# Three more pairs of projection blocks with seven-product units in a hybrid mixer layer on Trainium2

## The chip, the core and the metric

One core of one Trainium2 chip runs the whole layer in one launch. The metric is the device time in microseconds, the median of repeated runs: 2087.34 us before the change.

## What is computed

The reference is one decoder layer on 256 rows of 2048 columns, in float32:

```
h = x
f1 = (silu(n(h) @ w_gate) * (n(h) @ w_up)) @ w_down      # 2048 -> 5504 -> 2048
h = h + 0.5 * rms_norm(f1)
u = rms_norm(h); proj = u @ w_in                          # 11 parts of w_in's columns
g_q, g_k, g_v, g_out, g_code, h_q, h_f, h_i, h_out, z_gla, z_hgrn = split(proj)
o_gla  = gated_linear_attention(g_q, g_k, g_v, decay(g_code)) * silu(g_out)     # 4 heads
o_hgrn = gated_linear_attention(silu(h_q), 1 - f, h_i, f(h_f)) * silu(h_out)    # 8 heads
merged = sigmoid(z_gla) * (o_gla @ w_branch_gla) + sigmoid(z_hgrn) * (o_hgrn @ w_branch_hgrn)
h = h + rms_norm(merged @ w_out)
h = h + 0.5 * rms_norm(second feed-forward like the first)
```

## The kernel before

The 256 rows are two row blocks t of 128. Every product of float32 matrices is made of three passes in a reduced format (mm3, L145): high part by high part, low by high, high by low. Weights arrive in chunks of two 128-row tiles by 512 columns, by SyncE's (SP's) DMA queue, into a ring of five raw tiles; ScalarE (ACT) copies a chunk to its high part `whi` and VectorE (DVE) subtracts to get the low part `wlo` (split_into, L140), each in a ring of five. A plain 512-column block (`gemm_block`, L151) has eight chunks, each of twelve matmuls of 128x512 on TensorE (PE).

A pair (`gemm_pair`, L319) computes two blocks together. In some of its eight row-tile pairs ("units", `seven`, L255) it replaces eight 128-tile products by seven products of sums, 21 matmuls for 24; DVE forms the weights' sums (`wsum`, `wsuml`), ACT their high parts (`wsumh`). At the end of a pair, shared products are added up (`share`) and added to the results (`close`, L307). A pair occupies all eight PSUM banks once its seven-product units have begun, four for results c and four for shared products p.

The mixer's blocks come in this order before: GQ; CODE with HQ0 (528 columns); the pairs GK/GV0 and GV1/GO0; the plain blocks GO1, HF0, HI0, HO0, HQ1, HF1, HI1, HO1; ZG0, BG0 (branch product of the first attention), ZG1, BG1; the pair ZG2/ZG3 and BG2, BG3; two pairs of ZH; four branch blocks of the second attention; then the output projection. First letters: G and H are the two branches' parts, Z the branch gates.

Other work is put between chunks by a `Side` object (L41): after each twelve matmuls `pump` takes one step of every light generator (transposes, decays `hfT`/`hkT`, dot products `hd`) and, at every second pump, one step of each of the first two heavy ones, the attention chains of t = 0 and 1. An attention chain goes through levels of 1 to 64 rows: small matmuls of qT and kT on PE (L885, L892), then scalings of kT and qT and a masked copy on DVE (L901 to L906), later matmuls with the values, a copy of the state on ACT (L955) and normalised, gated outputs (L967). The attention chains of a branch are appended when its values and gates exist. Every engine runs its instructions in the order that the program fixes; PE's matmuls of a plain chunk stand there as hi, lo, hi passes in turn.

The residual h stays in eight SBUF tiles. After the first layer's settle of h (L492) the mixer reads it again only at its end.

Of the kernel before, what the change touches and what calls it, by code (L numbers as in the profile page):

```python
# [7 lines left out]
F32 = mybir.dt.float32  # L8
# [19 lines left out]
RW = -(-2 * (16 + CB) * 4 // LINE) * LINE // 4  # L28
# [12 lines left out]
class Side:  # L41
# [5 lines left out]

    def __init__(self):
        self.light, self.heavy, self.due = [], [], False

    def _step(self, queue, g):
        try:
            next(g)
        except StopIteration:
            queue.remove(g)
# [5 lines left out]
    def pump(self):  # L61
        for g in list(self.light):
            self._step(self.light, g)
        self.due = len(self.heavy) < 2 or not self.due
        if self.due:
            for g in self.heavy[:2]:
                self._step(self.heavy, g)
# [12 lines left out]
def kernel(ctx: ExitStack, tc: tile.TileContext, a: dict, out: bass.AP):  # L80
# [10 lines left out]
    psum = ctx.enter_context(tc.tile_pool(name="psum", bufs=8, space=bass.MemoryType.PSUM))  # L91

# [9 lines left out]
    h = [[hpool.tile([P, CB], F32, name=f"h{t}_{n}") for n in range(4)] for t in range(NT)]  # L102

# [47 lines left out]
    def gemm_block(w_dram, c0, w, lhs, nkt=KT, held=None, raws=(), ready=()):  # L151
# [5 lines left out]
        nb = -(-w // CB)  # L157
        pss = [[ps_tile(f"mm{t}") for _ in range(nb)] for t in range(NT)]

        def chunk(k0, alloc):  # L160
            if ready:
                return ready.pop(0)
            raw = raws.pop(0) if raws else None
            return wchunk(w_dram[k0 * P:(k0 + 2) * P, c0:c0 + w].rearrange("(k p) c -> p k c", p=P),
                          w, alloc, raw)

        def mm(t, k0, parts):
            for i, part in enumerate(parts):
                kt = k0 + i
                x = lhs(t, kt)  # L170
                for j, ps in enumerate(pss[t]):
                    sl = slice(j * (w // nb), (j + 1) * (w // nb))
                    mm3(ps[:, :w // nb], x, (part[0][:, sl], part[1][:, sl]),
                        kt == 0, kt == nkt - 1)

        if held is None:
            for k0 in range(0, nkt, 2):
# [22 lines left out]
    def operand_sums(x, new_part, out, more=True):  # L200
# [4 lines left out]
        for units in [SUMS] + [(u,) for u in FOUR if more and u not in SUMS]:  # L205
            n = len(units)
# [112 lines left out]
    def gemm_pair(ws, w, lhs, sums, ready=(), following=(), raws=(), sevens=SUMS):  # L319
# [15 lines left out]
        if len(sevens) > len(SUMS):  # L335
# [6 lines left out]
        for u, i in steps:  # L342
# [12 lines left out]
        for i in range(2 if sevens else 0):  # L355
            for t in range(NT):
                b.close(t, i)
        return *[[b.c[t][i] for t in range(NT)] for i in range(2)], ready
# [409 lines left out]
    def mixer(x, rs, ready, following):  # L768
        xl = lhs_of(x)
        w_in = a["w_in"]  # L770
        with ExitStack() as mctx:
# [5 lines left out]
            def blk(s, dt=F32):  # L777
                return b2.tile([P, CB], dt, tag="b", name=nm(s), bufs=31)
# [31 lines left out]

            def transposed(src, dst):
# [4 lines left out]
                nc.scalar.copy(dst, tp)  # L816

            def scaled(ps, sc, s):
                dst = blk(s)
# [8 lines left out]
            def gate(ps, r, normw, width, s):  # L828
                sg = silu(ps, r, blk(s))
# [13 lines left out]
            def dots(q, k, d, row=None):  # L843
# [3 lines left out]
                pr = blk("pr")  # L847
                if row is not None:
                    nc.vector.tensor_tensor(pr, q, row(), op=ALU.mult)
                    q = pr  # L850
                nc.vector.tensor_tensor(pr, q, k, op=ALU.mult)
                nc.vector.tensor_reduce(d, tiles4(pr), AX.X, ALU.add)
# [7 lines left out]
            def attention(t, qT, kT, fT, d, vs, gates, dv, br, b0):  # L860
# [3 lines left out]


# [69 lines left out]
                for b in range(nb):  # L935
                    while t == 1 and (br, b0 + b) not in state:
                        yield
                    o = ps_tile()
                    for j in range(hpb):
# [3 lines left out]
                                         rhs=vs[b][:, cs], start=True, stop=t == 0)  # L943
# [3 lines left out]
                    if t == 0:  # L947
                        kv = ps_tile()
                        for j in range(hpb):
# [3 lines left out]
                                             rhs=vs[b][:, cs], start=True, stop=True)  # L953
# [11 lines left out]
                    for j in range(hpb):  # L965
                        cs = slice(j * dv, (j + 1) * dv)
                        nc.vector.scalar_tensor_tensor(on[:, cs], o[:, cs], r[:, j:j + 1],  # L967
                                                       gates[b][:, cs], op0=ALU.mult, op1=ALU.mult)
# [14 lines left out]
            def branch_bias(row, n):  # L983
                bt = blk("bg")
# [4 lines left out]
            def branch_gate(z, bt):  # L989
                sz = []  # L990
                for t in range(NT):
                    s = blk("sz")
                    nc.vector.scalar_tensor_tensor(s, z[t], rs[t], bt, op0=ALU.mult, op1=ALU.add)
                    nc.scalar.activation(s, s, AF.Sigmoid)
                    sz.append(s)
                return sz

            def gla_decays(code, fT):
# [35 lines left out]
                for g, m in enumerate(ms):  # L1034
                    mv = m.rearrange("p (h t c) -> p h t c", t=NT, c=P)
                    for t in range(NT):
                        nc.scalar.activation(tiles4(fT[t])[:, 2 * g:2 * g + 2, :], mv[:, :, t, :],
                                             AF.Exp)

            def hgrn_gates(y, t, g, fT, kT):  # L1040
# [6 lines left out]
                for i in range(4):  # L1047
# [5 lines left out]
                    lc[:, 4 * g:4 * g + 4].unsqueeze(2).broadcast_to([P, 4, P]), op=ALU.mult)  # L1053

# [24 lines left out]
            def two(sums, c0, c1, ready, *following):  # L1079
# [3 lines left out]
                                 sevens=FOUR if four else SUMS)  # L1083
# [44 lines left out]
            k, v, ready = two(sums, O_GK, O_GV, (), cols(O_GV + CB), cols(O_GO))  # L1128
# [3 lines left out]
            vb, gb = [[scaled(v[t], rs[t], "v") for t in range(NT)]], []  # L1132
            v, go, ready = two(sums, O_GV + CB, O_GO, ready, cols(O_GO + CB))
            vb.append([scaled(v[t], rs[t], "v") for t in range(NT)])
            gb.append([gate(go[t], rs[t], gnorm, 256, "go") for t in range(NT)])
            go = gemm_block(w_in, O_GO + CB, CB, xl, ready=ready)
            gb.append([gate(go[t], rs[t], gnorm, 256, "go") for t in range(NT)])
            for t in range(NT):
# [172 lines left out]
```

## Time and profile before

| quantity | value |
|---|---|
| median of 3 runs | 2087.34 us (2087.27 to 2087.7) |
| profiled execution | 2087.65 us, its span 2085.7 us, mean granted clock 0.999 |
| PE busy | 2075.6 us |
| DVE busy | 1790.7 us, 86% |
| ACT busy | 1207.8 us, 58% |
| weight traffic | 195 GB/s over the span |

The span is the time from the first instruction to the last in the trace; some 2 us of the run's time lie around it. Matmul ends are modelled in the trace, so consecutive start times tell the pace, and a PE that is called busy may still wait inside a row.

### The profile page before, as it was taken

The page shows a single profiled execution, that of the slowest core. Times are in us where ns is not written, and L with a number is a line of the kernel's source. Part 1 is how long each engine was busy: PE and PEld are TensorE (multiplying, and loading weights), DVE is VectorE, ACT ScalarE, POOL GpSimd, SP SyncE. Part 2 cuts the span into 40 slices and gives each one's busy share as a digit, 9 for nine tenths or more (in the row PEclk, how much of TensorE's full clock was granted, in tenths as well). Part 3 has the DMA queues.
Part 4 walks back from the last instruction along what each step waited for, and adds up shares of the span by engine and source line. Part 5 has one row for each costly group of instructions (what it writes and reads, how often), then busy time and mean ns, then how long its engine had stood idle before and what let it go on. Part 6 is the DMA issues. An engine that isn't in the chain of part 4 may idle for free.

```text
span 2085.7 us, 29137 instructions
## 1 busy us (share of the span) xinstructions
PE 2075.6 (100%) x10553; PEld 1730.5 (83%) x10553; DVE 1790.7 (86%) x2116; ACT 1207.8 (58%) x1594; POOL 38.4 (2%) x87
## 2 busy tenths in 40 slices
PE   9999999999999999999999999999999999999998
PEld 7888888898888888888888888888888888898886
DVE  7898999989999889766668897578999989999896
ACT  6555656565666576554545564465655555566563
POOL 1000000000000100000000000010000000000000
PEclk9999999999999999999999999999999999999999
DMA  8566656667667456655565675655655656575663
GB/s 266 184 209 200 213 187 197 209 185 222 216 198 234 150 180 201 183 152 163 167 177 171 214 229 191 207 189 172 219 190 191 208 191 217 166 244 192 204 212 128
DMA packets 198034, 408.22 MB, mean 196 GB/s; under 512 B 17201, under 2 KB 25841, under 8 KB 197890
## 3 DMA queue, kind: packets, MB, share of 16 engines
q1 hardware_dynamic: 193136, 399.70, 61.0%
q10 hardware_dynamic: 4754, 6.66, 1.0%
q8 instruction: 82, 1.34, 0.3%
q14 instruction: 62, 0.51, 0.1%
HBM read 404.20 MB, written 2.10 MB: 195 GB/s over the span
## 4 chain that ended last, share of the span: by engine, by line
PE 97%; DVE 1%; issue 0%; ACT 0%; DMA 0%; POOL 0%; DVEq 0%; POOLq 0%; ACTq 0%
PE c L147 19%; PE c L149 19%; PE c L148 19%; PE mm L147 6%; PE mm L149 6%; PE mm L148 6%; PE p L148 5%; PE p L149 5%; PE p L147 5%; PE ps L379 2%; PE acc L149 1%; PE acc L147 1%; PE acc L148 1%; DVE h L492 0%; PE ps L885 0%
## 5 line engine op out<-in xcount | busy, mean ns | idle before, releaser
L141 ACT ACTIVATE whi<-raw 128x1024 fp32r<-128x1024 f32 (+3 forms) x520 | 541.7, 1048 | 367.7 <-PE mm L148 153.6
L143 DVE TENSOR_TENSOR wlo<-raw,whi 128x1024 fp32r<-128x1024 f32 (+3 forms) x520 | 624.0, 1208 | 145.7 <-ACT whi L141 137.4
L147 PE MATMUL c<-whi,xhi 128*128 128x512 f32 (+1 forms) x1055 | 408.8, 388 | 0.0
L149 PE MATMUL c<-wlo,xhi 128*128 128x512 f32 (+1 forms) x1055 | 406.2, 385 | 0.0
L148 PE MATMUL c<-whi,xlo 128*128 128x512 f32 (+1 forms) x1055 | 406.2, 385 | 0.0
L233 DVE TENSOR_TENSOR wlo<-raw,whi 128x1024 fp32r<-128x1024 f32 (+1 forms) x222 | 259.3, 1201 | 7.8 <-ACT whi L272 4.3
L149 PEld LDWEIGHTS c<-wlo,xhi 128*128 128x128 f32 x1055 | 198.1, 188 | 38.3
L147 PEld LDWEIGHTS c<-whi,xhi 128*128 128x128 f32 x1055 | 198.1, 188 | 37.6 <-ACT xhi L451 0.5
L148 PEld LDWEIGHTS c<-whi,xlo 128*128 128x128 f32 x1055 | 198.2, 188 | 37.3
L233 DVE TENSOR_TENSOR wsuml<-wsum,wsumh 128x1536 fp32r<-128x1536 f32 (+1 forms) x111 | 191.8, 1728 | 36.3 <-ACT wsumh L274 35.9
L147 PE MATMUL c<-whi,hkhi 128*128 128x512 f32 x558 | 217.0, 389 | 0.0
L149 PE MATMUL c<-wlo,hkhi 128*128 128x512 f32 x558 | 216.8, 388 | 0.0
L148 PE MATMUL c<-whi,hklo 128*128 128x512 f32 x558 | 216.7, 388 | 0.0
L272 ACT ACTIVATE whi<-raw 128x1024 fp32r<-128x1024 f32 (+1 forms) x111 | 116.0, 1045 | 169.9 <-DVE raw L233 55.3
L147 PE MATMUL mm<-whi,xhi 128*128 128x512 f32 (+1 forms) x456 | 174.9, 384 | 0.0
L268 ACT ACTIVATE whi<-raw 128x1024 fp32r<-128x1024 f32 (+1 forms) x111 | 115.7, 1042 | 97.9 <-PE c L148 88.3
L149 PE MATMUL mm<-wlo,xhi 128*128 128x512 f32 (+1 forms) x456 | 171.3, 376 | 0.0
L148 PE MATMUL mm<-whi,xlo 128*128 128x512 f32 (+1 forms) x456 | 171.0, 375 | 0.0
L270 ACT ACTIVATE wsumh<-wsum 128x1024 fp32r<-128x1024 f32 (+1 forms) x111 | 115.7, 1042 | 91.0 <-DVE wsum L233 61.8
L233 DVE TENSOR_TENSOR wsum<-raw,raw 128x1024 f32<-128x1024 f32 (+1 forms) x111 | 133.6, 1203 | 20.7 <-DMA raw<-in_ffn_w_down_dram 15.4
L149 PEld LDWEIGHTS c<-wlo,hkhi 128*128 128x128 f32 x558 | 104.8, 188 | 21.6
L147 PEld LDWEIGHTS c<-whi,hkhi 128*128 128x128 f32 x558 | 104.8, 188 | 21.4
(340 smaller groups left out, 3221.5 us busy)
## 6 DMA issues: line engine op xcount, KB each, us to landing
raw<-in_w_in_dram SPq DMA_DIRECT2D x134, 512.0 KB, 3.8
raw<-in_ffn_w_down_dram SPq DMA_DIRECT2D x124, 512.0 KB, 4.8
raw<-in_ffn_w_up_dram SPq DMA_DIRECT2D x97, 512.0 KB, 4.6
raw<-in_ffn_w_gate_dram SPq DMA_DIRECT2D x96, 512.0 KB, 4.7
raw<-in_ffn_w_gate_dram SPq DMA_DIRECT2D x128, 256.0 KB, 3.8
raw<-in_ffn_w_up_dram SPq DMA_DIRECT2D x126, 256.0 KB, 4.0
raw<-in_ffn_w_down_dram SPq DMA_DIRECT2D x96, 256.0 KB, 4.4
raw<-in_w_in_dram SPq DMA_DIRECT2D x68, 256.0 KB, 3.0
```

The source lines that it names most:

```text
L141: last[0] = nc.scalar.activation(hi, src, AF.Copy)
L143: nc.vector.tensor_tensor(lo, src, hi.bitcast(F32), op=ALU.subtract)
L147: nc.tensor.matmul(ps, lhsT=xhi, rhs=whi, start=start, stop=False)
L148: nc.tensor.matmul(ps, lhsT=xlo, rhs=whi, start=False, stop=False)
L149: nc.tensor.matmul(ps, lhsT=xhi, rhs=wlo, start=False, stop=stop)
L233: return nc.vector.tensor_tensor(o, x, y, op=op)
L268: nc.scalar.activation(ahi, ra, AF.Copy)
L270: nc.scalar.activation(hi[:, 0:2, :], wsum[:, 0:2, :], AF.Copy)
L272: nc.scalar.activation(bhi, rb, AF.Copy)
L379: end = nc.tensor.transpose(dst_ps[:, i * P:(i + 1) * P], src[:, i * P:(i + 1) * P], ident)
```

## The change

Three pairs more are made of plain blocks: GO1 with HF0, HI1 with HO1, ZG0 with ZG1. Each has three seven-product units (of the operand sums that exist already), at the steps 6, 8 and 10 of the pair's (`late=True`), so that attention can use PSUM banks in the steps before. In such a pair `side.fast` makes heavy steps come at every pump, and `side.full` stops them once a seven-product unit is next or running. HI0, HO0, HQ1, HF1 stay plain. The pair GO1/HF0 is followed by HI0 with one chunk prepared (`cols(O_HI)`).

Attention chains are appended before their values and gates exist (`attend`); a chain yields `WAITS`, which is not counted as a step, until its inputs are marked as written (`laid`) and until the values and gates of its next part are there. The operand sums for the pairs of four units are formed once more only for the unit that was missing.

To make room, the residual is stored to DRAM (`away`, eight stores of 256 KB on SP's queue, behind GQ's loads and among the first of CODE's), its tiles serve for gates, values and biases meanwhile, and eight loads on ACT's queue bring it back in `merge`. The raw ring's tiles shrink from 1088 to 1024 columns: CODE is loaded and split in sixteen chunks of one 128-row tile by 528. The dot products and gates are formed in place, `blk` has 33 buffers for 31.

Counts: PE issues 27 matmuls of 128x512 fewer; DVE has 56 instructions more (nine seven-product units, three `share`, twelve `close` against what was removed), ACT 34 and SP 34 more.

```diff
+RW = 2 * CB
     def pump(self):
...
+        self.due = self.fast or len(self.heavy) < 2 or not self.due
+        if self.due and not self.full:
+            steps = 0
+            for g in list(self.heavy):
+                steps += self._step(self.heavy, g) != Side.WAITS
+                if steps == 2:
+                    break
...
     def gemm_pair(...)
+        if late:
+            at = range(6, 6 + 2 * len(sevens), 2)
...
+            side.fast = late
+            if any(i is None for _, i in steps[j:j + 2]):
+                side.full = True
...
     def attention(...)
+                while not all(id(x) in laid for x in (qT, kT, fT, d)):
+                    yield Side.WAITS
...
-                    while t == 1 and (br, b0 + b) not in state:
-                        yield
+                    while (t == 1 and (br, b0 + b) not in state) or b >= min(len(vs), len(gates)):
+                        yield Side.WAITS
...
+            for t in range(NT):
+                for n in range(4):
+                    nc.sync.dma_start(away[t][n], h[t][n])
...
+            vs, gates = attend(qT, kT, fT, dd, 256, "g", 0)
...
-            go = gemm_block(w_in, O_GO + CB, CB, xl, ready=ready)
+            go, f, ready = two(O_GO + CB, O_HF, ready, cols(O_HI), late=True)
+            gates.append([gate(go[t], rs[t], gnorm, 256, h[t][len(gates)]) for t in range(NT)])
...
+            vs, gates = hgrn(0, hqs, hqT, f)
+            side.spawn(lc_row(1))
+            vs.append(values(gemm_block(w_in, O_HI, CB, xl, ready=ready), 0))
...
+            v, go, ready = two(O_HI + CB, O_HO + CB, (), cols(O_ZG), cols(O_ZG + CB), late=True)
...
+            szs, ready = two_gates(0, O_ZG, 0, ready, first_of(a["w_branch_gla"], 0), late=True)
...
+                nc.scalar.dma_start(m, away[t][n])
```

**The order on the engines.** Each row is line, operation, result <- operands, shape; the line numbers of the changed program are some 10 to 30 higher. First DVE's queue before, at the start of HI0: `wlo` is the low part of a weight chunk, `lcl` part of the next group's row of bounds, `hfT`/`hkT` are decays and keys of the second branch, `pr` and `hd` its dot products.

```order
L143 TENSOR_TENSOR wlo_8171<-raw_8168,whi_8170 128x1024
L1063 SCALAR_TENSOR_TENSOR lcl_7964<-ident,lc,lch_7963 128x128 x4
L143 TENSOR_TENSOR wlo_8189<-raw_8186,whi_8188 128x1024
L1049 TENSOR_SCALAR hfT_7949<-hfT_7949,lc,lb 128x128 x4
L1051 TENSOR_TENSOR hkT_7951<-hkT_7951,lc 128x512
L1049 TENSOR_SCALAR hfT_7950<-hfT_7950,lc,lb 128x128 x4
L1051 TENSOR_TENSOR hkT_7952<-hkT_7952,lc 128x512
L849 TENSOR_TENSOR pr_8017<-hq_6432,lcr_6845 128x512
L849 TENSOR_TENSOR pr_8021<-hq_6433,lcr_6845 128x512
L851 TENSOR_TENSOR pr_8017<-pr_8017,hk_7957 128x512
L851 TENSOR_TENSOR pr_8021<-pr_8021,hk_7959 128x512
L852 TENSOR_REDUCE hd_7961<-pr_8017 128x4
```

In the change DVE's queue at the start of HI0, from the row after the first `hfT` and `hkT`; `kT`/`qT` are scaled for the attention of the first branch, and `wlo_8271` is the low part of HI0's third chunk.

```order
L1076 TENSOR_SCALAR hfT_8138<-hfT_8138,lc,lb 128x128 x4
L1078 TENSOR_TENSOR hkT_8140<-hkT_8140,lc 128x512
L874 TENSOR_TENSOR hk_8145<-hk_8145,lcr_6911 128x512
L872 TENSOR_TENSOR hk_8147<-hq_6443,hk_8147 128x512
L875 TENSOR_REDUCE hd_8149<-hk_8145 128x4
L874 TENSOR_TENSOR hk_8147<-hk_8147,lcr_6911 128x512
L928 TENSOR_TENSOR kT_7219<-kT_7219,tot_7611 128x8x32
L875 TENSOR_REDUCE hd_8150<-hk_8147 128x4
L931 TENSOR_TENSOR qT_6438<-qT_6438,tot_7611 128x8x32
L928 TENSOR_TENSOR kT_7220<-kT_7220,tot_7633 128x8x32
L931 TENSOR_TENSOR qT_6439<-qT_6439,tot_7633 128x8x32
L153 TENSOR_TENSOR wlo_8271<-raw_8268,whi_8270 128x1024
```

The two splits that stood ahead of the decays are down to one (further up, ahead of `lcl`); the products are now in `hk`; attention's scalings and then the split of HI0's third chunk come behind them all.

PE's queue in the same place of the change, from the end of HI0's second chunk: `whi_8270` and `wlo_8271` are the parts of the third chunk, `L919` the small matmuls of attention's levels 32 and 64.

```order
L1097 MATMUL ps_8223<-lcl_8152,ones 128x512
L919 MATMUL ps_8228<-qT_6438,kT_7219 32x32 x8
L919 MATMUL ps_8248<-qT_6439,kT_7220 32x32 x8
L157 MATMUL mm_1699_8161<-whi_8270,xhi_1311_6092 128x512
L158 MATMUL mm_1699_8161<-whi_8270,xlo_1312_6093 128x512
L157 MATMUL mm_1700_8162<-whi_8270,xhi_1326_6187 128x512
L158 MATMUL mm_1700_8162<-whi_8270,xlo_1327_6188 128x512
L919 MATMUL ps_8304<-qT_6438,kT_7219 64x64 x4
L919 MATMUL ps_8311<-qT_6439,kT_7220 64x64 x4
L159 MATMUL mm_1699_8161<-wlo_8271,xhi_1311_6092 128x512
```

Before, the twelve matmuls of a chunk stood together there; now four high passes are taken out ahead, and the matmuls of level 64, which read what DVE scaled, stand ahead of the first low pass.

The second place is ACT's queue at the state copy of the second branch's first group, before (in the block HO0 to HQ1) and in the change (in the pair HI1/HO1). `whi` is the high part of a weight chunk.

```order
L141 ACTIVATE whi_9449<-raw_9447 128x1024
L933 COPY ke_9316<-ps_9311 128x512
L141 ACTIVATE whi_9467<-raw_9465 128x1024
L141 ACTIVATE whi_9503<-raw_9501 128x1024
L955 COPY state_9364<-ps_9359 128x512
L961 ACTIVATE sq_9366,oss_9367<-ps_9354 128x128 x4
```

```order
L151 ACTIVATE whi_9519<-raw_9517 128x1024
L1072 ACTIVATE hfT_9254<-ps_9290 128x512
L1073 ACTIVATE hkT_9256<-ps_9290 128x512
L1072 ACTIVATE hfT_9255<-ps_9302 128x512
L1073 ACTIVATE hkT_9257<-ps_9302 128x512
L982 COPY state_9324<-ps_9319 128x512
```

Ahead of the copy of the state stood weight copies; now a weight copy and the four activations of the next group's decays do.

## Rows read from the trace of the kernel before

**Rows 1.** The page of the profiled execution: busy time of each engine with its share of the span, and the chain that ended last, by engine.
```profile
PE 2075.6 (100%) x10553; PEld 1730.5 (83%) x10553; DVE 1790.7 (86%) x2116; ACT 1207.8 (58%) x1594; POOL 38.4 (2%) x87
...
PE 97%; DVE 1%; issue 0%; ACT 0%; DMA 0%; POOL 0%; DVEq 0%; POOLq 0%; ACTq 0%
```

**Rows 2.** Timeline of TensorE in the pair GK/GV0, the first matmul of a seven-product unit and the first after its 21: start us, duration us, line, matmul.
```profile
757.95 0.39 PE L147 MATMUL p<-whi,xhi 128*128 128x512 f32 x1
...
762.71 0.39 PE L147 MATMUL c<-whi,xhi 128*128 128x512 f32 x1
```

**Rows 3.** Busy time by windows: stretch, its length, then PE, PEld, DVE, ACT, POOL busy us (instructions), granted clock, DMA share, GB/s. The mixer's projections from GK to the end of the branches; the pair GV1/GO0; a pair of the first feed-forward layer with four seven-product units.
```profile
743.20:1304.40 561.20, 561.19 (x3577) 462.20 (x3576) 441.68 (x613) 311.61 (x459) 12.15 (x22) 1.00 0.61 184
786.90:830.90 44.00, 44.00 (x199) 36.53 (x199) 40.12 (x42) 27.82 (x39) 0.00 (x0) 1.00 0.63 197
181.60:222.20 40.60, 40.60 (x184) 33.68 (x183) 38.90 (x39) 23.06 (x27) 0.00 (x0) 1.00 0.60 192
```

**Rows 4.** Timeline of ScalarE in the plain block HF0, with what ended the idle time ahead of it.
```profile
863.53 1.06 ACT L141 ACTIVATE whi<-raw 128x1024 fp32r<-128x1024 f32 x1 [1.66 <-PE mm L148]
```

**Rows 5.** Groups of instructions in 743.2 to 1304.4 us: line, engine, operation, shape, count | busy us, mean ns | idle before.
```profile
L233 DVE TENSOR_TENSOR wsuml<-wsum,wsumh 128x1536 fp32r<-128x1536 f32 x16 | 28.0, 1753 | 7.7 <-ACT wsumh L274 7.6
L233 DVE TENSOR_TENSOR wsum<-raw,raw 128x1024 f32<-128x1024 f32 x16 | 19.5, 1221 | 1.2 <-DMA raw<-in_w_in_dram 0.9
L233 DVE TENSOR_TENSOR c<-c,psum 128x512 f32<-128x512 f32 x20 | 13.0, 690 | 0.0
L233 DVE TENSOR_TENSOR psum<-psum,p 128x512 f32<-128x512 f32 (+1 forms) x15 | 12.9, 859 | 0.3
L233 DVE TENSOR_TENSOR raw<-wsum,raw 128x512 f32<-128x512 f32 x16 | 11.0, 691 | 0.4
```

**Rows 6.** Timeline of DVE after the pair GV1/GO0: closes, weight splits, gates.
```profile
830.41 1.41 DVE L233 TENSOR_TENSOR c<-c,psum 128x512 f32<-128x512 f32 x2
...
834.60 1.40 DVE L825 SCALAR_TENSOR_TENSOR go<-c,r,go 128x512 f32<-128x512 f32 x2
...
837.12 2.35 DVE L143 TENSOR_TENSOR wlo<-raw,whi 128x1024 fp32r<-128x1024 f32 x2
```

**Rows 7.** Timeline of ScalarE at the start of HI0.
```profile
877.19 0.67 ACT L820 ACTIVATE y<-mm,r 128x512 f32<-128x512 f32 x1
...
879.98 1.05 ACT L141 ACTIVATE whi<-raw 128x1024 fp32r<-128x1024 f32 x1
880.92 0.58 ACT L1045 ACTIVATE hfT<-ps 128x512 f32<-128x512 f32 x1
```

**Rows 8.** Timeline of DVE at the start of HI0, in the order of its queue.
```profile
879.62 1.13 DVE L1063 SCALAR_TENSOR_TENSOR lcl<-ident,lc,lch 128x128 fp32r<-128x128 f32 x4
...
882.20 1.12 DVE L1049 TENSOR_SCALAR hfT<-hfT,lc,lb 128x128 f32<-128x128 f32 x4
...
885.56 1.28 DVE L849 TENSOR_TENSOR pr<-hq,lcr 128x512 f32<-128x512 f32 x2
...
887.97 1.26 DVE L852 TENSOR_REDUCE hd<-pr 128x4 f32<-128x512 f32 x2
889.16 0.41 DVE L901 TENSOR_TENSOR kT<-kT,tot 128x256 f32<-128x256 f32 x1
889.49 0.41 DVE L904 TENSOR_TENSOR qT<-qT,tot 128x256 f32<-128x256 f32 x1
...
890.76 1.21 DVE L143 TENSOR_TENSOR wlo<-raw,whi 128x1024 fp32r<-128x1024 f32 x1
891.89 0.41 DVE L901 TENSOR_TENSOR kT<-kT,tot 128x256 f32<-128x256 f32 x1
```

**Rows 9.** Timeline of one early attention step in HF0 (PE, then DVE), and the transposes of 743.2 to 1304.4 as a group.
```profile
863.65 0.74 PE L885 MATMUL ps<-qT,kT 128*32 128x16 f32 x64
864.18 0.42 DVE L901 TENSOR_TENSOR kT<-kT,fT 128x256 f32<-128x256 f32 x1 [1.04 <-PE ps L885]
...
865.79 1.22 DVE L143 TENSOR_TENSOR wlo<-raw,whi 128x1024 fp32r<-128x1024 f32 x1
...
L379 PE MATMUL ps<-ident,on 128*128 128x128 f32 x32 | 4.3, 272 | 0.0
```

**Rows 10.** Timeline around a state copy of the second branch: the state's matmuls on PE, and the matmuls that use its copy.
```profile
1010.88 1.06 PE L952 MATMUL ps<-hv,ke 128*128 128x128 f32 x8
...
1012.71 0.40 PE L945 MATMUL ps<-state,hqT 128*128 128x128 f32 x2
```

**Rows 11.** The last settle of the residual on DVE and the first matmul of CODE on PE.
```profile
701.47 0.74 DVE L492 SCALAR_TENSOR_TENSOR h<-c,r,h 128x512 f32<-128x512 f32 x1
...
718.77 0.28 PE L147 MATMUL mm<-whi,xhi 128*128 128x264 f32 x1
```

**Rows 12.** TensorE's first matmuls, one at the usual pace, its last matmul, and two windows after it (columns as in the table of windows; the granted clock is the third figure from the end).
```profile
1.29 4.21 PE L1251 MATMUL ps<-idle 128*128 128x512 f32 x9 [1.29 <-POOL idle L1246]
...
9.39 0.39 PE L149 MATMUL c<-wlo,xhi 128*128 128x512 f32 x1
...
2076.85 0.39 PE L149 MATMUL c<-held,hkhi 128*128 128x512 f32 x1
...
2081.00:2082.00 1.00, 0.00 (x0) 0.00 (x0) 1.00 (x3) 0.00 (x0) 0.00 (x0) 1.00 0.60 225
2082.00:2083.00 1.00, 0.00 (x0) 0.00 (x0) 0.51 (x1) 0.00 (x0) 0.00 (x0) 0.80 1.02 379
```

More of the change, by code (lines that the diff above doesn't have):

```diff
@@ L41 @@
 class Side:
+    WAITS = "waits"
     def __init__(self):
-        self.light, self.heavy, self.due = [], [], False
+        self.light, self.heavy, self.due, self.full = [], [], False, False
+        self.fast = False
     def _step(self, queue, g):
         try:
-            next(g)
+            return next(g)
         except StopIteration:
@@ L102 @@
     h = [[hpool.tile([P, CB], F32, name=f"h{t}_{n}") for n in range(4)] for t in range(NT)]
+    away = [[dram.tile([P, CB], F32, name=f"away{t}_{n}") for n in range(4)] for t in range(NT)]
     nhalf = const.tile([P, 4], F32, name="nhalf")
@@ L157, in gemm_block @@
         nb = -(-w // CB)
+        step = 2 // nb
         pss = [[ps_tile(f"mm{t}") for _ in range(nb)] for t in range(NT)]
@@ L205, in operand_sums @@
         for units in [SUMS] + [(u,) for u in FOUR if more and u not in SUMS]:
+            if units[0] in out:
+                continue
             n = len(units)
@@ L317, in first_of, with gemm_pair @@
         return chunk
-    def gemm_pair(ws, w, lhs, sums, ready=(), following=(), raws=(), sevens=SUMS):
+    def gemm_pair(ws, w, lhs, sums, ready=(), following=(), raws=(), sevens=SUMS,
+                  late=False):
         raws = list(raws)
@@ L357, in gemm_pair @@
                 b.close(t, i)
+        side.full = side.fast = False
         return *[[b.c[t][i] for t in range(NT)] for i in range(2)], ready
@@ L809, in mixer, with mark @@
                 rq.append(r)
+            laid = set()
+            def mark(*tiles):
+                laid.update(id(x) for x in tiles)
             def transposed(src, dst):
@@ L983, in branch_bias @@
             def branch_bias(row, n):
-                bt = blk("bg")
+                bt = blk("sz") if row else h[0][n]
                 nc.scalar.dma_start(
@@ L987, in branch_bias, with branch_gate @@
                 return bt
[L989 to L995, printed above, removed]
+            def branch_gate(z, bt, s=None):
+                sz = [bt, s or blk("sz")]
+                for t in (1, 0):
+                    nc.vector.scalar_tensor_tensor(sz[t], z[t], rs[t], bt, op0=ALU.mult, op1=ALU.add)
+                    nc.scalar.activation(sz[t], sz[t], AF.Sigmoid)
                 return sz
@@ L1038, in gla_decays @@
                                              AF.Exp)
+                mark(*fT)
             def hgrn_gates(y, t, g, fT, kT):
@@ L1077, in cols, with two @@
                 return first_of(w_in, c0)
-            def two(sums, c0, c1, ready, *following):
+            def two(c0, c1, ready, *following, late=False):
                 four = len(sums) > len(SUMS) and c1 != O_ZH + 3 * CB
                 return gemm_pair([(w_in, c0), (w_in, c1)], CB, xl, sums, ready, following,
-                                 sevens=FOUR if four else SUMS)
+                                 sevens=FOUR if four else SUMS, late=late)
             qs = [scaled(q[t], rq[t], "q") for t in range(NT)]
@@ L1126, in mixer, with attend @@
             side.spawn(lc_row(0))
-            k, v, ready = two(sums, O_GK, O_GV, (), cols(O_GV + CB), cols(O_GO))
+            def attend(qT, kT, fT, dd, dv, br, b0):
+                vs, gates = [], []
+                for t in range(NT):
+                    side.heavy.append(attention(t, qT[t], kT[t], fT[t], dd[t], vs, gates, dv, br, b0))
+                return vs, gates
+            for t in range(NT):
+                for n in range(4):
+                    nc.sync.dma_start(away[t][n], h[t][n])
+            k, v, ready = two(O_GK, O_GV, (), cols(O_GV + CB), cols(O_GO))
             ks = [scaled(k[t], rs[t], "k") for t in range(NT)]
```

126 lines of the change are left out of this document (59 added, 67 removed).

## The prediction

> **What bounds the kernel now.** The page's first part and its chain say TensorE (PE): it is busy for the whole span and holds 97% of the chain [rows 1]. That view cannot show slack, so I went on to start times. In a seven-product unit the first of 21 matmuls of 128x512 starts at 757.95 and the next unit's first at 762.71: (762.71 - 757.95)/21 = 0.227 us each [rows 2]; a plain chunk of twelve takes 2.72 us. No view of PE's waits names anything in mid-kernel, so each matmul taken out is worth 0.227 us, as long as the other engines keep up. The table of windows tells how near they are: in the mixer's projections VectorE (DVE) works 441.68 of 561.20 us, but 40.12 of 44.00 in the pair GV1/GO0 [rows 3]. What keeps PE fed through DVE's uneven work is a lead: the weight copies on ScalarE (ACT) wait for PE to give back a ring slot [rows 4], so four chunks, 4 x 2.72 = 10.9 us, lie split ahead of PE in a plain block.
>
> **The change part by part.** *Fewer matmuls.* Three pairs with three seven units each save 3 x 3 x 3 = 27 matmuls (24 products become 21 in a unit): 27 x 0.227 = 6.1 us. This is on the path everywhere.
>
> *More DVE work.* A unit adds a sum, two half sums and a long split: 1.22 + 2 x 0.69 + 1.75 = 4.35 us [rows 5]; nine are 39.2. Twelve closes at 0.69 are 8.3, nine sums of shared products at 0.86 are 7.7: 55.2 us in all, less one formation of operand sums. It hides beside PE: 441.68 + 55.2 is still below 561.20 less 6.1. So on average nothing is lost; a loss can only come where DVE's work bunches up and the lead is short.
>
> *Place one, the start of HI0.* A pair uses up the lead: its last closes on DVE wait for its last matmul on PE. Call that moment E. After the pair GO1/HF0 comes HI0, with one chunk split at E and the rest behind other work. DVE's queue (first place of the order) is, from the end of the last close at E + 0.8: two gates (four instructions, 834.60 to 837.12, 2.52) [rows 6], the split of the second chunk 1.13, the four lcl 1.13, and one hk product 0.60 [rows 8], which makes E + 6.2. ACT delivers what these need in time: after a weight copy (1.05) and the first y (0.67) its second y, hk and lch take 877.19 to 879.98, 2.8, and a weight copy and hfT, 879.98 to 881.50, another 1.5 [rows 7]: E + 6.0. Then follows what stood together in the kernel before from 882.20 to 890.76 [rows 8]: the decays, 882.20 to 885.56, 3.36; the other three of four products, which took 885.56 to 887.97, 1.8; two reductions to 889.16, 1.2; and four scalings of an attention level at 0.33, 1.3. That is 7.7, so E + 13.9; and only then comes the split of chunk three, 1.13 (890.76 to 891.89): E + 15.0. In the kernel before the same group held up no one: its 8.6 us lay under the lead of 10.9. Now PE has, after E, chunk one 2.72, chunk two 2.72 and a third of chunk three 0.91, eight transposes at 4.3/32 = 0.13, two ones-products at 0.23 and 16 small matmuls of attention, of which 64 took 0.74 [rows 9], some 1.8 more: 8.2, and with its bubbles it stands at about E + 8.4 before matmuls that need those scalings, and then before the split. The wait is 15.0 - 8.4 = **6.6 us**. Bounds: 3 if DVE is a chunk earlier, 8 if the second chunk's split is late too. I take 6.6, since every term is a row of the same instruction.
>
> *The state copy.* In the pair HI1/HO1 the small matmuls that use the attention state follow the copy of it on ACT. Before, 1.83 us from 1010.88 to 1012.71 were enough from the state's own matmuls to the first that uses the copy, and PE filled them [rows 10]; now a weight copy and four activations stand ahead of it on ACT (second place of the order): 1.05 + 4 x 0.58 = 3.4 us [rows 7]. PE's work in between covers what it did and some more; I take 1.3 of it as uncovered (0 to 3.4). The first branch's state stands behind one weight copy and one activation: 0.6 (0 to 1.6).
>
> *Attention inside the pairs.* Late pairs take a step of both chains at every chunk until the units come, 1.6 us of DVE by the rows from 864.18 to 865.79 [rows 9], beside the previous pair's gates and closes. The second step in GO1/HF0 and the one in ZG0/ZG1 each reach PE before DVE has scaled: 0.8 and 0.85 (0 to 2.7, one chunk). At the start of GK/GV0 and of BG0 I find 0.3 each.
>
> *What is hidden.* The residual goes to DRAM on SP's queue, eight stores, ahead of most weight loads of CODE. They wait for the settles of h, done at about 702.2 [rows 11]; CODE starts on PE at 718.8 [rows 11], 16 us later, and only its first two half chunks are loaded ahead of the last stores. No row shows such a store; eight of 256 KB at the 184 GB/s of the mixer [rows 3] would fill 11.4 us, less than the 16, so I cost them at nothing (0 to 3, a chunk, if they start late). The reloads on ACT's queue come with the merge, which ends with the branches at 1304; the residual is used from 1383.7 on. CODE in sixteen half chunks has the same matmuls, and the products in place the same operations.
>
> *Sum.* -6.1 + 6.6 + 1.3 + 0.6 + 0.8 + 0.85 + 0.6 = +4.65. The profiled execution (2087.65, of which 2085.7 span) is 0.3 above the median of 2087.34; put on the median, 2087.34 + 4.65 gives **2092.0 us**. The bounds of the waits, 3 (HI0 alone) to 8 + 3.4 + 1.6 + 2.7 + 2.7 + 0.6 = 19, give 2084 to 2100. A difference of 0.2% (4.2 us) is about what a measurement of this kernel can tell.
>
> **The rivals.** *The clock falls in the HI0 wait.* At the end of the kernel PE's last matmul starts at 2076.85, and the granted clock is 1.00 in each row to 2082 and 0.80 in the next [rows 12]; that is an idle time as long as the 5.5 us that PE would spend before its small matmuls at HI0. [...] At the kernel's start nine matmuls take 4.21 us, 0.47 each in place of 0.227 [rows 12], and by 9.39 they are at full rate; half rate over 4 to 6 us costs 2 to 3. That gives 2094 to 2097. Against it: the wait is at the edge, and is broken by the eight small matmuls.
>
> *Only the large wait is real; not slower.* The waits besides HI0 (4.15 in sum) each hang on PE reaching one copy or scaling within a chunk of it. One queue decides them: if ACT holds its copies when PE frees the slot, as [rows 4] show in plain blocks, PE's preceding chunk (2.72) covers them all. Then 2087.34 - 6.1 + 6.6 = 2087.8. The deciding point is a sum of waits of 6.1 + 4.2 = 10.3: mine is 10.75, so little is needed. With HI0's wait at its lower bound too, 2085.
>
> *The cover holds.* If DVE kept its splits ahead at HI0, as it did before with the same 8.6 us, only some small waits would be left: 2081 to 2084, faster. For it: the four-seven pair runs at 38.90 us of DVE in 40.60 with no wait [rows 3]. Against it: in that pair's block nothing but splits follows the closes, and DVE runs its queue in the order written.
>
> *DVE becomes the bound of the new pairs,* or the trip of h delays weights: the GV1/GO0 pair's 40.12 of 44.00 plus a third unit's 4.35 exceeds what PE takes; every pair could lose 1 to 4 us beyond the lead it enters with: above 2097.
>
> **How the numbers follow.** Forecast (2089.5 to 2094.5, centre 2092) 0.40; clock falls 0.18; only the large wait 0.25; cover holds 0.12; DVE bound 0.05. Faster by over 0.2% (below 2083.2) is most of the cover's case: 0.12. Slower by over 0.2% (above 2091.5) is 0.24 of the forecast's 0.40, the clock's 0.18 and DVE's 0.05: 0.47. The rest, 0.41, is within. The range 2083.5 to 2096.5 leaves out about 0.1 below and 0.08 above.
>
> **What would show it.** In the changed profile, 27 fewer 128x512 matmuls; at the start of HI0 a gap of 5 us or more in PE's start times, with DVE busy on hfT, hkT, hk and hd, and no weight split for some 10 us; a gap of about 1 us before the state's matmuls in HI1/HO1; the granted clock at 1.00 beside the gap (the forecast) or lower behind it (the rival). Wrong would be: no gap at HI0, which leaves only the saved 6.1; or gaps spread over the pairs with DVE at 100%.

## The result and the profile after

| | before | after |
|---|---|---|
| median of 12 runs each | 2087.61 us (2087.27 to 2088.11) | 2092.18 us (2091.0 to 2093.08) |
| ratio after to before | | 1.0021, 95% interval 1.0013 to 1.0029 |
| profiled execution, its span | 2087.65, 2085.7 us | 2091.0, 2089.2 us |

The change makes the kernel slower by 4.6 us; 2092.0 had been forecast. The profiled execution of after is the shortest of its twelve runs, so the trace shows a little less than the usual loss.

The page's first part shows PE busy for less time, DVE for more, both in a longer span [rows 1]:

```profile
PE 2073.3 (99%) x10526; PEld 1725.2 (83%) x10526; DVE 1834.0 (88%) x2172; ACT 1219.7 (58%) x1620; POOL 38.2 (2%) x87
```

The windows of after (columns as in [rows 3]): the mixer's stretch, DVE now 486.36 where it was 441.68, and then the start of HI0 cut where PE's state changes.

```profile
743.20:1304.40 561.20, 555.20 (x3535) 454.94 (x3535) 486.36 (x664) 323.41 (x476) 12.09 (x22) 1.00 0.61 188
...
887.50:892.00 4.50, 0.26 (x2) 0.08 (x2) 4.50 (x10) 4.36 (x15) 0.00 (x0) 1.00 0.00 0
892.00:893.00 1.00, 0.92 (x12) 0.81 (x13) 1.00 (x3) 0.98 (x5) 0.00 (x0) 0.89 0.03 8
893.00:896.00 3.00, 2.96 (x12) 2.34 (x11) 3.00 (x5) 0.59 (x2) 0.00 (x0) 0.50 0.34 65
896.00:897.00 1.00, 1.00 (x5) 0.84 (x4) 1.00 (x2) 0.00 (x0) 0.00 (x0) 0.90 1.07 387
```

PE works 0.26 us in the 4.5 us from 887.5, DVE all of them; afterwards the granted clock reads 0.89, 0.50 and 0.90; behind 897 it is 1.00 again. PE's timeline there (start, duration, line, matmul) shows the same:

```profile
878.76 0.39 PE L157 MATMUL mm<-whi,xhi 128*128 128x512 f32 x1
...
887.29 0.40 PE L158 MATMUL mm<-whi,xlo 128*128 128x512 f32 x1
891.92 1.77 PE L919 MATMUL ps<-qT,kT 128*64 128x64 f32 x16 [4.24 <-DVE qT L931]
893.73 0.80 PE L159 MATMUL mm<-wlo,xhi 128*128 128x512 f32 x1
894.32 0.63 PE L157 MATMUL mm<-whi,xhi 128*128 128x512 f32 x1
894.75 0.63 PE L158 MATMUL mm<-whi,xlo 128*128 128x512 f32 x1
...
896.34 0.39 PE L158 MATMUL mm<-whi,xlo 128*128 128x512 f32 x1
```

878.76 is E of the prediction, the first matmul of HI0. The last high pass ahead of the wait starts at 887.29 and is over for the pace at 887.52, E + 8.8 (8.4 forecast); the small matmuls of level 64 start at 891.92; the first low pass, which needs `wlo_8271`, starts at 893.73, E + 15.0 (15.0 forecast). From 894.32 to 896.02 matmuls start 0.43 us apart, behind 896.34 0.23 us. DVE's queue in the same stretch is the list of the forecast, with the answers to [rows 6] and [rows 8]:

```profile
878.96 0.70 DVE L243 TENSOR_TENSOR c<-c,psum 128x512 f32<-128x512 f32 x1 [0.45 <-PE c L159]
879.57 1.40 DVE L849 SCALAR_TENSOR_TENSOR h<-c,r,h 128x512 f32<-128x512 f32 x2
...
882.08 1.22 DVE L153 TENSOR_TENSOR wlo<-raw,whi 128x1024 fp32r<-128x1024 f32 x1
883.22 1.13 DVE L1091 SCALAR_TENSOR_TENSOR lcl<-ident,lc,lch 128x128 fp32r<-128x128 f32 x4
884.27 0.68 DVE L872 TENSOR_TENSOR hk<-hq,hk 128x512 f32<-128x512 f32 x1
884.87 1.11 DVE L1076 TENSOR_SCALAR hfT<-hfT,lc,lb 128x128 f32<-128x128 f32 x4
...
887.52 0.68 DVE L1078 TENSOR_TENSOR hkT<-hkT,lc 128x512 f32<-128x512 f32 x1
888.13 0.68 DVE L874 TENSOR_TENSOR hk<-hk,lcr 128x512 f32<-128x512 f32 x1
...
890.53 0.41 DVE L928 TENSOR_TENSOR kT<-kT,tot 128x256 f32<-128x256 f32 x1
...
892.13 0.41 DVE L931 TENSOR_TENSOR qT<-qT,tot 128x256 f32<-128x256 f32 x1
892.46 2.35 DVE L153 TENSOR_TENSOR wlo<-raw,whi 128x1024 fp32r<-128x1024 f32 x2
```

Lines left out are of the same kinds. The reader is to see that each instruction begins as the one ahead of it ends (to within 0.1 us), and that no split of a weight chunk stands between 882.08 and 892.46. The view of PE's waits (line, what it waited for, us, times, longest) names the rest; before, it named the start of the kernel alone:

```profile
PE ps L919 <- DVE qT L931: 4.2, 1, 4.2
...
PE ps L972 <- ACT state L982: 0.8, 1, 0.8
PE p L157 <- ACT lcr L1099: 0.7, 1, 0.7
PE ps L397 <- DVE hq L849: 0.2, 1, 0.2
```

Two of them stand where the forecast had little or nothing: 0.7 behind the copy of `lcr` on ACT (in the pair GK/GV0), and 0.8 at a state copy (in a branch block, not in HI1/HO1).

### The profile page after: what moved, and what is told of

It is laid out like the page before. It is cut to its first block, busy times and chain, and to the rows that moved or that the text cites. A ratio compares the mean times of both kernels' runs of the same rounds, so it can differ in the third digit from the quotient of the medians.

```text
span 2089.2 us, 29267 instructions
## 1 busy us (share of the span) xinstructions
PE 2073.3 (99%) x10526; PEld 1725.2 (83%) x10526; DVE 1834.0 (88%) x2172; ACT 1219.7 (58%) x1620; POOL 38.2 (2%) x87
## 4 chain that ended last, share of the span: by engine, by line
PE 96%; DVE 2%; DMA 1%; issue 1%; ACT 0%; POOL 0%; SPq 0%; DVEq 0%; POOLq 0%; ACTq 0%
PE c L157 21%; PE c L159 21%; PE c L158 21%; PE p L157 5%; PE p L159 5%; PE p L158 5%; PE mm L159 4%; PE mm L157 4%; PE mm L158 4%; PE ps L397 2%; PE acc L157 1%; PE acc L159 1%; PE acc L158 1%; DVE wlo L153 1%; PE ps L912 0%
## 5 line engine op out<-in xcount | busy, mean ns | idle before, releaser
L153 DVE TENSOR_TENSOR wlo<-raw,whi 128x1024 fp32r<-128x1024 f32 (+3 forms) x510 | 602.6, 1191 | 113.5 <-ACT whi L151 111.7
L157 PE MATMUL c<-whi,xhi 128*128 128x512 f32 (+1 forms) x1184 | 461.0, 390 | 0.1
L159 PE MATMUL c<-wlo,xhi 128*128 128x512 f32 (+1 forms) x1184 | 457.0, 386 | 0.0
L158 PE MATMUL c<-whi,xlo 128*128 128x512 f32 (+1 forms) x1184 | 456.7, 386 | 0.0
L159 PEld LDWEIGHTS c<-wlo,xhi 128*128 128x128 f32 x1184 | 222.3, 188 | 43.9 <-DVE wlo L153 0.3
L157 PEld LDWEIGHTS c<-whi,xhi 128*128 128x128 f32 x1184 | 222.3, 188 | 42.8 <-ACT xhi L469 0.6
L158 PEld LDWEIGHTS c<-whi,xlo 128*128 128x128 f32 x1184 | 222.4, 188 | 42.2 <-issue 0.3
L158 PEld LDWEIGHTS c<-whi,hklo 128*128 128x128 f32 x558 | 104.7, 188 | 21.5
L157 PE MATMUL mm<-whi,xhi 128*128 128x512 f32 (+1 forms) x264 | 98.7, 374 | 0.0
L159 PE MATMUL mm<-wlo,xhi 128*128 128x512 f32 (+1 forms) x264 | 96.9, 369 | 0.0
```

The source lines that it names most:

```text
L153: nc.vector.tensor_tensor(lo, src, hi.bitcast(F32), op=ALU.subtract)
L157: nc.tensor.matmul(ps, lhsT=xhi, rhs=whi, start=start, stop=False)
L158: nc.tensor.matmul(ps, lhsT=xlo, rhs=whi, start=False, stop=False)
L159: nc.tensor.matmul(ps, lhsT=xhi, rhs=wlo, start=False, stop=stop)
```

## The experiments

Every run stands beside runs of the kernel before on the same chip, whose median was 2087.7 to 2087.8. The intervals of the ratios are some 0.0009 to either side (2 us), so a difference under 2 us between two runs rests on the traces as much as on the times. E stands below for the first matmul of HI0 of the run in question.

**Is it the order at HI0?** The dot products of the second branch's first group are taken two (t = 0) and four pumps (t = 1) later; nothing else changes:

```diff
-            def dots(q, k, d, row=None):
+            def dots(q, k, d, row=None, later=0):
                 yield
                 yield
+                for _ in range(later):
+                    yield
...
+                for j, (q, k, d) in enumerate(zip(qs, ks, ds)):
+                    side.spawn(dots(q, k, d, row, 2 * j + 2 if s == "hd0" else 0))
```

> All three pairs stay; the dot products of the second branch's first group (four products, two reductions, 3.6 us of DVE) are taken two and four pumps later. Theory A: the order of DVE's queue is the whole matter; the split of HI0's third chunk comes by E + 5.7 and that of the fourth by E + 11.6, where PE arrives at about E + 11.1, so the wait falls from 6.2 to under 1 us and the clock stays at full rate: 2083.5 to 2085.5. Theory B: DVE has the same work, so the wait moves to the next chunks or to HO0: 2090 or more.

Measured: 2085.77 us, ratio to before 0.9991 [0.9982, 1.0000], 6.4 us less than the change itself. On DVE the split of chunk three now precedes the decays, and PE's twelve matmuls of that chunk run on. DVE's and then PE's timeline of this run:

```profile
882.11 1.22 DVE L153 TENSOR_TENSOR wlo<-raw,whi 128x1024 fp32r<-128x1024 f32 x1
...
884.30 1.22 DVE L153 TENSOR_TENSOR wlo<-raw,whi 128x1024 fp32r<-128x1024 f32 x1
885.43 1.11 DVE L1078 TENSOR_SCALAR hfT<-hfT,lc,lb 128x128 f32<-128x128 f32 x4
...
889.70 0.42 DVE L933 TENSOR_TENSOR qT<-qT,tot 128x256 f32<-128x256 f32 x1
890.03 1.22 DVE L153 TENSOR_TENSOR wlo<-raw,whi 128x1024 fp32r<-128x1024 f32 x1
```

```profile
889.96 0.39 PE L158 MATMUL mm<-whi,xlo 128*128 128x512 f32 x1
890.28 1.15 PE L921 MATMUL ps<-qT,kT 128*64 128x64 f32 x16
891.35 0.50 PE L159 MATMUL mm<-wlo,xhi 128*128 128x512 f32 x1
```

The small matmuls wait 0.1 us and the low pass comes right behind them. The whole loss at HI0 is gone with the same work on DVE: the order is the cause, and the rival that the wait would only move on falls. No view of PE's waits names HI0 any more. The time is 0.3 above theory A's range; the waits that are left in mid-kernel are 1.1 at a state copy, 0.7 behind `lcr` and 0.2 for `hq`. More of them below.

**Taking more out of the way.** As above, with the dot products four and six pumps later and the decays of both row blocks later as well:

```diff
+                    side.spawn(dots(q, k, d, row, 2 * j + 4 if s == "hd0" else 0))
...
             def hgrn_gates(y, t, g, fT, kT):
                 yield
+                for _ in range(2 * t + 1 if g == 0 else 0):
+                    yield
```

> All three pairs stay; the dot products come four and six pumps later, the decays of t = 0 one pump and of t = 1 three pumps later. Theory A: no wait at HI0 at all; 2083 to 2085, no better than the run with late dot products alone by more than 0.5 us. Theory B: 2090 or more, since the same DVE work has to be done before HO0 ends.

Measured: 2085.87 us, 0.9992 [0.9983, 1.0000]. That is 0.9 above theory A's range, but no better than the run before it, as theory A said and far from theory B: with the dot products out of the way nothing was left to win at HI0.

**What is the clock's part?** Seventeen matmuls are put on PE where it stands idle:

```diff
+                    if br == "g" and t == 0 and c == 64:
+                        warm = ps_tile("warm")
+                        for _ in range(17):
+                            nc.tensor.matmul(warm, lhsT=ones, rhs=x[0][0][:, 0:4, :]...)
```

> Seventeen extra matmuls of 128x512 into a spare PSUM tile stand on PE where it waits at HI0, 17 x 0.227 = 3.9 us of the 4.4 us gap; their result is not used. Theory A with the lower clock as a part of the loss: the granted clock stays at 1.00 after the wait, the 1.3 us of half-rate matmuls (more in most runs, by their lower mean clock) is won back: 2089.5 to 2091, and the runs differ by less than the 2 us they differ by in the changed kernel. Rival (the clock costs nothing): 2092, or 2092 to 2093 if the extra matmuls get in the way.

Measured: 2090.78 us (2089.88 to 2091.43), 1.0012 [1.0004, 1.0021], 1.4 us less than the change. The timeline of PE and the windows of this run:

```profile
888.75 4.13 PE L909 MATMUL warm<-xhi,ones 128*128 128x512 f32 x17
893.17 1.32 PE L924 MATMUL ps<-qT,kT 128*64 128x64 f32 x16 [0.29 <-DVE qT L936]
894.88 0.50 PE L159 MATMUL mm<-wlo,xhi 128*128 128x512 f32 x1 [0.40 <-DVE wlo L153]
895.22 0.39 PE L157 MATMUL mm<-whi,xhi 128*128 128x512 f32 x1
```

```profile
892.00:893.00 1.00, 0.88 (x4) 0.38 (x2) 1.00 (x4) 1.00 (x5) 0.00 (x0) 1.00 0.00 0
893.00:896.00 3.00, 2.42 (x21) 2.02 (x22) 3.00 (x6) 1.81 (x8) 0.00 (x0) 1.00 0.03 8
```

The low pass waits as before for DVE's split, but the clock reads 1.00 from 892 to 896, where it was 0.89 and then 0.50 in the change, and the matmuls behind the wait start 0.23 us apart from 895.22 on, where the change's start 0.43 apart. By the medians of these two runs the clock costs 1.4 us of the 6.4, DVE's order 5. The difference of 1.4 lies within the intervals, so the traces decide: from E to the first matmul of HI1/HO1 the change takes 114.73 us (878.76 to 993.49), this run 113.62 (879.87 to 993.49) and the run with late dot products 108.49 (878.78 to 987.27). By them the clock costs 1.1 and the order 5.1. The profiled execution of this run is as long as that of the change all the same (2091.1 and 2091.0 us), since it lost 1.1 us ahead of E, where the two kernels are the same. In the trace of the change 4.4 us pass from 887.52 to 891.92, and 1.81 us to the low pass where the run with late dot products takes 1.07: again 5.1 for the order. The runs spread over 1.6 us where the change's spread over 2.1, which is no clear difference.

**The first pair undone.** GO1 and HF0 are plain blocks:

```diff
-            go, f, ready = two(O_GO + CB, O_HF, ready, cols(O_HI), late=True)
+            go = gemm_block(w_in, O_GO + CB, CB, xl, ready=ready)
...
+            vs, gates = hgrn(0, hqs, hqT, gemm_block(w_in, O_HF, CB, xl))
```

> GO1 and HF0 are plain blocks again; the pairs HI1/HO1 and ZG0/ZG1, the early attention and the residual's trip stay. Theory A (the loss is one wait at the start of HI0, made by DVE's queue behind a pair with one chunk split, and the lower clock after it): the wait of 6.2 us and some 1.3 to 2.5 us of half-rate matmuls go, 9 matmuls (2.0 us) come back, so 2085.5 to 2086.5 and no gap over 1 us at HI0. Theory B (the new pairs give DVE more work than fits, the wait only shows first at HI0): a gap of several us opens in a later block and the time stays above 2090.

Measured: 2087.8 us, 1.0002 [0.9993, 1.0010]. The wait at HI0 is gone, though DVE's burst is not: 11.4 us pass there from one weight split to the next, more than the 10.4 (882.08 to 892.46) of the change. DVE's timeline:

```profile
884.58 1.23 DVE L153 TENSOR_TENSOR wlo<-raw,whi 128x1024 fp32r<-128x1024 f32 x1 [1.50 <-ACT whi L151]
...
896.00 1.22 DVE L153 TENSOR_TENSOR wlo<-raw,whi 128x1024 fp32r<-128x1024 f32 x1
```

Behind plain blocks the chunks that lie split ahead of PE cover it. So the short lead behind the pair is as much a part of the cause as the order: take away either, and the wait is gone. The time, however, is 1.3 above the upper end of theory A's range. The trace names one reason, a wait that the change does not have, in the pair HI1/HO1: the first small matmuls of the second branch's second group wait there for DVE (timeline of DVE, ScalarE and PE):

```profile
1004.10 0.67 DVE L875 TENSOR_REDUCE hd<-hk 128x4 f32<-128x512 f32 x1
1004.69 1.28 DVE L897 TENSOR_TENSOR hqT<-hqT,hfT 128x512 f32<-128x512 f32 x2
...
1005.51 0.45 PE L912 MATMUL ps<-hqT,hkT 128*32 128x16 f32 x32 [1.45 <-DVE hqT L897]
```

In the change the same matmuls stand in the same pair, but later: they start at 1012.78, 6 us behind DVE's scaling at 1006.19. Without the first pair the first group's attention begins sooner (932.46 for 947.16), and the second group's then comes right behind the scaling. So a wait in a later block, of which theory B spoke, did come, but of 1.5 us and not of several. Without that 1.5 the time would lie in theory A's range.

**What does each other pair bring?** On top of the late dot products, HI1/HO1 and then ZG0/ZG1 are made plain again:

```diff
-            v, go, ready = two(O_HI + CB, O_HO + CB, (), cols(O_ZG), cols(O_ZG + CB), late=True)
-            vs.append(values(v, 1))
-            gates.append(gates_of(go, 1))
+            vs.append(values(gemm_block(w_in, O_HI + CB, CB, xl), 1))
+            gates.append(gates_of(gemm_block(w_in, O_HO + CB, CB, xl), 1))
+            ready = ()
```

> As the run with late dot products (2085.8), but HI1 and HO1 are plain blocks. Theory A: the pair costs no wait of its own, so nine matmuls come back and nothing else: 2085.8 + 2.0 = 2087.8. Theory B (pairs filled with attention steps are bound by DVE): part of the 2.0 was never won, 2086 to 2087.

Measured: 2086.79 us, 0.9995 [0.9986, 1.0004], 1.0 more than with the pair, in theory B's range.

```diff
-            szs, ready = two_gates(0, O_ZG, 0, ready, first_of(a["w_branch_gla"], 0), late=True)
...
+            for i in range(2):
+                szs.append(branch_gate(gemm_block(w_in, O_ZG + i * CB, ...), bts[i], h[1][i]))
...
```

> As the run with late dot products (2085.8), but ZG0 and ZG1 are plain blocks. Theory A: nine matmuls come back, and the wait for the state copy near the branch block (1.2 us there) stays or falls with the new place of the attention steps: 2086.6 to 2087.8. Theory B: 2085.5 to 2086.5.

Measured: 2086.57 us, 0.9994 [0.9985, 1.0003], 0.8 more than with the pair, between the ranges of the two theories. In both traces PE's wait at the second branch's state copy, 1.1 us with late dot products, is gone, and so it is in the run without the first pair; in the run without ZG0/ZG1 one of 0.6 at the first branch's state has come. So that wait stands only where all three pairs do, and what a plain block gives back is a wait for ScalarE; neither trace shows a pair that DVE holds up. For HI1/HO1 2.0 - 1.1 = 0.9 fits the 1.0; for ZG0/ZG1 2.0 - 1.1 + 0.6 = 1.5 does not fit the 0.8. With intervals of 2 us the times do not settle what each pair brings.

**The other parts alone.** First the residual's trip and CODE's half chunks in the kernel before:

```diff
-RW = -(-2 * (16 + CB) * 4 // LINE) * LINE // 4
+RW = 2 * CB
...
+        step = 2 // nb
...
+                    nc.sync.dma_start(away[t][n], h[t][n])
...
+                nc.scalar.dma_start(h[t][n], away[t][n])
```

> The kernel before with only two parts of the change: the residual's trip to DRAM and back (its tiles are not used for anything else meanwhile) and CODE in sixteen half chunks with the smaller ring tiles. Prediction's theory: both are hidden, 2087.4 to 2088. Theory C, formed on the changed kernel's trace: the half chunks halve the lead that ScalarE has at the end of CODE, and the waits at the start of GK/GV0 (0.3 us for the transposes of hq, 0.85 us behind the copy of lcr) are theirs: 2088.4 to 2089.2, with both waits in the trace.

Measured: 2089.66 us, 1.0008 [0.9999, 1.0017], 0.5 above theory C's range and 1.7 above that of the prediction's theory. Of the two waits that theory C named, the one behind `lcr` is in the trace (1.0 us) and the one for the transposes of `hq` is not. Then the half chunks alone, the first two of these edits:

> The kernel before with CODE in sixteen half chunks and the smaller ring tiles alone, no trip of the residual. Theory C (the 1.9 us of the run with both parts are the half chunks': ScalarE enters GK/GV0 later and PE waits behind the copy of lcr): 2089.0 to 2089.8, with the wait of about 1.1 us at the fourth product of the first seven-product unit of GK/GV0. Rival D (the stores and reloads delay weight loads): 2087.5 to 2088, no such wait.

Measured: 2089.6 us, 1.0010 [1.0001, 1.0018], in theory C's range. And the trip alone, the last two:

> The kernel before with the residual's trip to DRAM and back alone, CODE in eight chunks as before. Theory C: hidden, 2087.5 to 2088. Rival D: 2089 to 2089.8.

Measured: 2087.6 us, 0.9999 [0.9990, 1.0008], in theory C's range. The trip is free as far as these times can tell, the half chunks cost 1.9 us. In the run with the half chunks ScalarE's queue is late from the end of CODE on (its last copy of CODE, the first high part of a weight sum, the row of `lcr`; then PE's wait):

```profile
735.68 0.65 ACT L141 ACTIVATE whi<-raw 128x528 fp32r<-128x528 f32 x1 [0.81 <-PE mm L148]
...
748.45 1.04 ACT L268 ACTIVATE wsumh<-wsum 128x1024 fp32r<-128x1024 f32 x1
...
759.47 1.28 ACT L1035 ACT_TABLE_LOAD   x1
...
762.01 0.56 ACT L1069 COPY lcr<-ps 128x512 f32<-128x512 f32 x1
```

```profile
PE p L147 <- ACT lcr L1069: 0.9, 1, 0.9
```

In the kernel before, the same work started 7.2, 10.3 and 1.8 us sooner:

```profile
728.45 1.09 ACT L141 ACTIVATE whi<-raw 128x1056 fp32r<-128x1056 f32 x1 [1.82 <-PE mm L148]
...
738.13 1.05 ACT L270 ACTIVATE wsumh<-wsum 128x1024 fp32r<-128x1024 f32 x1
...
757.67 1.28 ACT L1037 ACT_TABLE_LOAD   x1
...
760.21 0.56 ACT L1071 COPY lcr<-ps 128x512 f32<-128x512 f32 x1
```

GK starts on PE at the same time in both (743.2), so the loss arises behind CODE. In both ScalarE waits for PE to give back a ring tile; the ring of five now holds half as much of CODE, so its copies of CODE end later and the work behind them falls due later. The wait is 0.9, and PE's start times from 740 to 768 make 1.4 of the 1.5 us by which this run's span is longer; the rest of the median's 1.9 is not seen in the trace.

**All the rest without the pairs.** Early attention, half chunks, trip, work in place, with none of the three pairs (the three edits above together):

> The changed kernel with none of the three pairs: early attention, half chunks, the trip and everything formed in place stay, and PE issues all 27 matmuls of before. Theory A with C: the early attention in plain blocks costs little beyond the half chunks' 1.9, so 2089.5 to 2090.5, and the pairs' 6.1 us are offset only by the wait at HI0 with its clock. Rival E (attention that begins sooner costs waits of its own): 2091 or more.

Measured: 2089.45 us, 1.0009 [1.0000, 1.0018], within 0.1 of the lower end of theory A's range. Beside the 1.9 of the half chunks early attention costs nothing here; the rival falls. This run also tells what the pairs bring once the wait at HI0 is out of the way: with late dot products the three pairs are 3.7 us faster than none (2085.77 for 2089.45), where 27 matmuls are 6.1.

**Two more steps.** The row of bounds `lcr` is formed later, in the pair GO1/HF0 (on top of the late dot products):

```diff
-            side.spawn(lc_row(0))
...
+            side.spawn(lc_row(0))
             go, f, ready = two(O_GO + CB, O_HF, ready, cols(O_HI), late=True)
```

> As the run with late dot products (2085.8), and the row of bounds lcr of the first group is formed at the start of the pair GO1/HF0 in place of GK/GV0. Theory C: PE's wait of 0.85 us in GK/GV0 hangs on that copy's place in ScalarE's queue behind a table load and the decays, so it goes: 2084.9 to 2085.3. Rival: ScalarE itself is late there and PE waits for the next weight sum instead: 2085.6 to 2086.

Measured: 2084.86 us, 0.9987 [0.9978, 0.9996]: faster than the kernel before by 2.9 us, the lowest median of all runs, and at the lower end of theory C's range. The wait behind `lcr` no longer stands among PE's waits, but one behind `lch` (the high part of the bounds, at the start of HI0) has come:

```profile
PE ps L974 <- ACT state L984: 0.9, 1, 0.9
...
PE ps L397 <- DVE hq L849: 0.4, 1, 0.4
PE ps L1098 <- ACT lch L1092: 0.4, 1, 0.4
```

That this step brought the 0.9 between the two medians is not shown. From GK's first matmul to E this run takes 134.43 us (743.21 to 877.64) where the run with late dot products alone takes 135.43 (743.35 to 878.78), but from E to the first matmul of HI1/HO1 109.35 (to 986.99) where that one takes 108.49: in the traces nearly all that is won in the first stretch is lost in the second.

Then the second row of bounds is moved from HI0 to HO0:

```diff
-            side.spawn(lc_row(1))
...
+            side.spawn(lc_row(1))
             gates.append(gates_of(gemm_block(w_in, O_HO, CB, xl), 0))
```

> As the run with late dot products and the first row of bounds at GO1/HF0 (2084.9), and the second row of bounds is formed in HO0 in place of HI0. Theory A: the remaining 0.75 us of waits on lch and on the scalings at the start of HI0 go: 2084.0 to 2084.4. Rival: they are taken over by the next wait on ScalarE's copies, 2084.7 to 2085.1.

Measured: 2085.53 us, 0.9989 [0.9981, 0.9998]. Not better: above theory A's range, and 0.4 above the rival's too. In its trace the wait on `lch` is gone, and one of 0.5 us for a weight split at HI0 has come. The two runs cannot be told apart by their intervals.

## Why the prediction was right

*The sum.* +4.65 was forecast, +4.6 came. The runs give this account: half chunks +1.9 (the run with them alone), matmuls -6.1, HI0 with its clock +6.4 (the change less the run with late dot products), together +2.2; 2.4 are left. They come with the pairs, which bring 3.7 in place of the 6.1 that their matmuls are reckoned at. The traces show about 1 of it at the state copy and up to 1.3 as gaps, most of them beside attention's small matmuls (start-to-start times 0.06 to 0.15 us longer than usual for their form add up to 10.1 us from 740 to 1310, where before they made 8.8; with the half chunks alone they make 9.2, so 0.4 of it is theirs). Some 0.5 stays open.

*HI0* is right by its mechanism and nearly by each step: DVE's last close ended at E + 0.9 (0.8 forecast), the split at E + 14.9 (15.0), PE came at E + 8.8 (8.4). The wait alone was 5 where I had 6.6: I did not take off the small matmuls that PE does within it, and PE came 0.4 later. The gap in PE's start times was 4.6 (887.29 to 891.92), a little under the 5 that the prediction set as its sign.

*The clock* was a rival with a chance of 0.18 and a price of 2 to 3. It did fall, in the trace of the change between 892 and 897 (0.89, 0.50 and 0.90), but cost only 1.4 (the run with the extra matmuls; 1.1 by the traces). The prediction's own sign, the clock lower behind the gap, was thus the rival's. The pace of 0.23 us came back by 896.34, with PE at work from 891.92. Forecast and rival were both half true, and that their sum, 5 + 1.4 = 6.4, comes so near the 6.6 that the forecast put on the wait alone is luck.

*What failed* are the small terms. "What is hidden" said that CODE in half chunks "has the same matmuls" and put nothing on them: they cost 1.9. Of the 0.3 put "at the start of GK/GV0" a wait of 0.2 for `hq` came, and the 0.7 behind `lcr` was not foreseen. I priced PE's work and DVE's and did not ask what becomes of ScalarE's lead when its ring holds half as much work. The state copy in HI1/HO1 (1.3) and that of the first branch (0.6) did not hold up PE; a copy in a branch block did, behind the weight sums of the next pair (in the change ScalarE takes a sum's high part at 1107.93 and the copy at 1108.90), for 0.8 to 1.1. The steps of attention in GO1/HF0 and ZG0/ZG1 (0.8 and 0.85) gave no wait over 0.2 us. These terms were 4.15 in the forecast and 4.3 came, from other places: the sum is right partly by luck.

*The rival that is not slower* (only the large wait is real) failed since the small waits came after all, elsewhere; the cover did not hold; DVE bound none of the pairs.

*Two figures among the rivals* do not follow from the prediction's own terms: 2 to 3 for the clock on top of 2092 gives 2094 to 2095, not up to 2097, and the large wait at its lower bound gives 2087.34 - 6.1 + 3 = 2084.2, not 2085. The forecast does not hang on either.

## What to carry to other kernels

Count what is already prepared for PE at the moment when a block ends, and then walk the other engine's queue in the order written: a burst that a long lead had hidden turns into a wait when the block ahead of it spends the lead. Moving six instructions of DVE by two and four chunks was worth as much here (6.4 us measured) as 27 matmuls (6.1 us reckoned). And when a ring's tiles are made to hold less, price the lead of every engine that runs ahead through it, not only the work.

## What was unexpected of the hardware

In the trace of the change PE worked 0.26 us of the 4.5 us from 887.5, and the granted clock still read 1.00 there; it read 0.89 from 892 to 893, when small matmuls were running again, 0.50 to 896, 0.90 to 897 and 1.00 behind: here the fall struck the work that came after the wait. In the run with seventeen matmuls without use in the wait the clock read 1.00 from 892 to 896, and its median was 1.4 us below that of the change.
